# Moving the key transposes, the value order, the key weighting and the last gates of an mLSTM layer between slots

## The chip, the cores and the metric

The kernel runs on one core of a Trainium2 chip. The metric is the device time of one execution in microseconds (us). The engines are TensorE (PE for its matmuls, PEld for its weight loads), VectorE (DVE), ScalarE (ACT), GpSimd (POOL) and SyncE (SP, which issues the transfers). Each engine works through a queue of its own in order.

## The reference

The program is two layers of a diffusion backbone over 512 latent and 256 context tokens of width 1024. The first layer is attention, the second a bidirectional chunkwise mLSTM; a convolutional feed-forward block follows each. The change lies in the mLSTM alone:

```
qk, v, o, g = split(h @ w_in)
q, k = split(silu(dwconv(qk)))                 # 8 heads of 64; k is scaled by 64 ** -0.5
# per head and direction, chunk by chunk, with gates i, f and running maximum m:
s   = (q @ k.T) * exp(logw - m)
num = w_inter * (C @ q) + s @ v                # v has 128 columns a head
den = w_inter * (n @ q) + sum(s)
h   = num / max(|den|, exp(-m))
C   = decay * C + sum(w * v * k)               # the state; n likewise
# the context gives only the first state
out = (rmsnorm(h_forward + h_backward) * sigmoid(o)) @ w_out
```

## The kernel before

Every fp32 product is split into a high and a low part, so that each matrix product is three matmuls (high by high, and the two mixed ones). `split` makes the parts: ScalarE writes the high one, VectorE the low one.

The mLSTM (`odd`) first computes the gate projections and their scans, the projections of head pair 0 and the output gates of heads 0 and 1. Then a loop over 43 slots `k` interleaves the stages of eight heads. Here a token tile is 128 tokens; tiles 0 to 3 are latent, 4 and 5 are context.

- `m_intra(h)`, slot 4h: decay matmuls into a double bank ("exps"), eight exponentials on ScalarE, the score matmuls into bank T ("psT"), their product on VectorE, and the split into `Dh` and `Dl` (`Dl` on GpSimd).
- `m_state(h)`, slot 4h+2: GpSimd weights the transposed keys of the head (`kw`, from `kt`), they are split into `kh` and `kl`, 18 matmuls make the sums of the six token tiles (first the two context tiles, then 0, 1, 2, 3), two ScalarE copies and six VectorE steps make the states, and they are split into `Sh` and `Sl`.
- `m_inter(h, q)`, slot 4h+4+q: eight matmuls for token tile q, drained by two VectorE operations.
- `m_norm`, `m_scale`, `m_out`: slots 4h+7, 4h+8 and 4h+10; VectorE work, then four transposes into bank T and the product with the gate.

Between these the list `fill` places the projections of the next pairs hp = 1, 2, 3 (`proj`): `qk(0)`, the queries, at slot 8hp-5; `qk(1)`, the keys, at 8hp-3; and the values two token tiles at a time, `v(0)`, `v(2)`, `v(4)`, at 8hp-1, 8hp and 8hp+1. `qk(1)` ends with six transposes of the convolved and activated keys (`cy`) and their copy `kt`. The gates of heads 2 to 7 (`gate(h)`: 24 matmuls into bank U, then a tanh) are at slots 10, 12, 18, 20, 26 and 28. From slot 31 on the first output projection (`out_first`) fills in.

The written order gives the priorities. The framework that builds the queues may place an instruction ahead of earlier written ones that are not ready, and adds all waits; on the chip each queue then runs in its fixed order.

Buffers that matter: two double banks of tag "S" are shared by the decay products, the state, the inter results and the key transposes. The projections alternate between banks U and R. `kt`, `kw`, `kh`, `kl`, `Dh`, `Dl`, `Sh` have one buffer each. The values of two pairs fit at a time.

Of the kernel before, what the change touches and what calls it, by code (L numbers as in the profile page):

```python
# [9 lines left out]
F32 = mybir.dt.float32  # L10
# [10 lines left out]
NL, NX, T = 512, 256, 768  # L21
# [11 lines left out]
class Kernel:  # L33
# [838 lines left out]
    def odd(self, hh, hl, OT, RP, HP, xs):  # L872
        nc, i = self.nc, self.i
# [4 lines left out]
        oh = RP.tile([128, 16], F32R, tag="onehot", name="onehot")  # L878
# [14 lines left out]
        MX = RP.tile([128, NL], F32R, tag="MX", name="MX")  # L893
        Y, WI, EM = [RP.tile([128, NT, 2, 8], F32, tag=t, name=t) for t in ("Y", "WI", "EM")]
        SW = RP.tile([128, 6, 2, 8], F32, tag="SW", name="SW")
        DEC = RP.tile([128, 16, 3], F32, tag="DEC", name="DEC")

        QP = self.QP = self.tc.alloc_tile_pool(name="qk1", bufs=1, reuse_waits="tile")
# [13 lines left out]
        def proj(hp, pd):  # L912
            def qk(w01):
                ch, segs = ((hp, [(0, NL)]), (4 + hp, [(0, NL), (NL, NX)]))[w01]
                w = self.weights(i["w_mqk"][ch], KD, 128)
                yq = QP.tile([128, T], F32, tag="cy", name="cy", bufs=1)
                tiles = [QP.tile([128, NL], F32R, tag=f"{'qk'[w01]}{j}", name="qk", bufs=2 - w01) for j in range(2)]
                if w01:
                    pd["kl"] = self.kl
                pd["qk"[w01]] = tiles  # L920
                for t0, m in segs:
                    ps = self.B(pd["tags"])
                    self.fm([(ps[:, 0:m], t0, m)], w, H, KD)
                    y = yq[:, t0:t0 + m]
                    self.conv(y, [ps[:, 0:m]], [cw[:, j, ch:ch + 1] for j in range(3)], cbs[:, ch:ch + 1], [(0, m)])

                    th = QP.tile([128, NL], F32, tag="tmp", name="th", bufs=1)[:, 0:m]
                    nc.scalar.activation(th, y, AF.Tanh, scale=0.5)
                    nc.vector.scalar_tensor_tensor(y, th, 1.0, y, op0=ADD, op1=MUL)
                    for j, (a, b) in enumerate(((slice(0, 64), slice(64, 128)), (slice(64, 128), slice(0, 64)))):  # L930
                        if t0:
                            break
                        t = tiles[j][:, t0:t0 + m]
                        if w01 == 0:
                            nc.scalar.mul(t[a], y[a], 0.5)
                            nc.vector.scalar_tensor_tensor(t[b], y[a], 0.5, f32(t[a]), op0=MUL, op1=SUB)
                        else:
                            nc.scalar.mul(t[a], y[a], 0.0625)
                            nc.gpsimd.tensor_scalar(t[b], y[a], 0.0625, 1.0, op0=MUL, op1=MUL)
                            nc.vector.scalar_tensor_tensor(self.kl[j][a, t0:t0 + m], y[a], 0.0625, f32(t[a]), op0=MUL, op1=SUB)  # L940
                if w01:

                    ps = self.A("kt")
                    for t in range(6):
                        nc.tensor.transpose(ps[:, t * 128:(t + 1) * 128], yq[:, t * 128:(t + 1) * 128], self.ident)
                    pd["kt"] = QP.tile([128, 6, 128], F32, tag="kt", name="kt", bufs=1)
                    nc.scalar.mul(pd["kt"].rearrange("p t c -> p (t c)"), ps[:, 0:T], 0.0625)

            def v(t):
                if t == 0:  # L950
                    pd["wv"] = self.weights(i["w_mv"][hp], KD, 256)

                    pd["v"] = [[QP.tile([128, 6, 130], F32R, tag=f"V{x}", name="V", bufs=4) for x in "hl"] for _ in range(2)]
                    for v2 in pd["v"]:
                        for x, val in zip(v2, (1.0, 0.0)):
                            nc.gpsimd.memset(f32(x[:, :, 128:130]), val)
                ps = self.B(pd["tags"])
                for e in range(2):
                    self.tm(ps[:, 256 * e:256 * e + 256], pd["wv"], H, KD, t + e)
                ps = ps.rearrange("p (t j c) -> p t j c", t=2, j=2)  # L960
                for j, (vh, vl) in enumerate(pd["v"]):
                    self.split(vh[:, t:t + 2, 0:128], vl[:, t:t + 2, 0:128], ps[:, :, j])

            return [lambda: qk(0), lambda: qk(1)] + [lambda t=t: v(t) for t in (0, 2, 4)]

        heads = [{} for _ in range(8)]

        def gate(h, tags="U"):
            ps = self.B(tags)
            self.fm([(ps, 0, NL)], self.weights(i["w_mo"][h], KD, 128), H, KD)  # L970
            t = heads[h]["gate"] = QP.tile([128, NL], F32, tag="gt", name="gt", bufs=3)
            nc.scalar.activation(t, ps, AF.Tanh, scale=0.5)

        with self.tc.tile_pool(name="gates", bufs=1, reuse_waits="tile") as GP:
# [9 lines left out]
            w = self.weights(i["w_mg"], KD, 128)  # L984
            ps = self.A("gates")
# [6 lines left out]
            pds = [dict(tags="UR" if hp else "TURO") for hp in range(4)]  # L992
# [31 lines left out]
            c = GP.tile([64, 6], F32, name="c")  # L1024
# [56 lines left out]
        fill = [[] for _ in range(43)]  # L1081
        for hp in range(1, 4):
            f = proj(hp, pds[hp])
            for c, w in ((-5, f[0:1]), (-3, f[1:2]), (-1, f[2:3]), (0, f[3:4]), (1, f[4:5])):
                fill[8 * hp + c] += w
        for h in range(2, 8):
            fill[4 * h + 2 - (h % 2) * 2].append(lambda h=h: gate(h))

        og = RP.tile([128, KD], F32, tag="og", name="og")
        nc.sync.dma_start(og, i["ml_og"])  # L1090
# [36 lines left out]

        dirs = [heads, pds, oh, MX, Y, WI, EM, SW, DEC]
        for k in range(43):
            for st, at in ((self.m_intra, 0), (self.m_state, 2)):  # L1130
                if k >= at and (k - at) % 4 == 0 and (k - at) // 4 < 8:
                    st((k - at) // 4, MP, *dirs)
            for f in fill[k]:
                f()
            q = k - 4
            if 0 <= q < 32:
                self.m_inter(q // 4, q % 4, MP, *dirs)
                if q % 4 == 3:
                    self.m_norm(q // 4, MP, *dirs)
            if q >= 4 and (q - 4) % 4 == 0 and (q - 4) // 4 < 8:  # L1140
                self.m_scale((q - 4) // 4, MP, *dirs)
            if q >= 6 and (q - 6) % 4 == 0 and (q - 6) // 4 < 8:
                self.m_out((q - 6) // 4, OT, *dirs)
# [30 lines left out]
            nc.gpsimd.tensor_tensor(wl[:, dr], w[:, dr], f32(wh[:, dr]), op=SUB)  # L1174
        heads[h]["w"] = (wh, wl)

    def m_state(self, h, pool, heads, pds, oh, MX, Y, WI, EM, SW, DEC):

        nc = self.nc
        pd, j = pds[h // 2], h % 2  # L1180
        a = slice(64 * j, 64 * j + 64)
        kw = pool.tile([128, 6, 2, 64], F32, tag="kw", name="kw", bufs=1)
        nc.gpsimd.tensor_tensor(kw, pd["kt"][:, :, a].unsqueeze(2).to_broadcast([128, 6, 2, 64]),
                                SW[:, :, :, h:h + 1].to_broadcast([128, 6, 2, 64]), op=MUL)
        kh, kl = [pool.tile([128, 6, 2, 64], F32R, tag=f"kw{x}", name="kw" + x, bufs=1) for x in "hl"]
        self.split(kh, kl, kw)
        vh, vl = pd["v"][j]
        ps = self.A("state")
        C = []
        for z, blocks in enumerate(((4, 5), (0,), (1,), (2,), (3,))):  # L1190
            c0 = z * 130 if z < 3 else 512 + (z - 3) * 130
            C.append(ps[:, c0:c0 + 130])
            m = 0
            for t in blocks:
                for x, y in ((kh, vh), (kl, vh), (kh, vl)):
                    nc.tensor.matmul(C[z], x[:, t].rearrange("p d c -> p (d c)"), y[:, t],  # L1196
                                     start=m == 0, stop=m == 3 * len(blocks) - 1)
                    m += 1
        S = pool.tile([64, 4, 2, 130], F32, tag="S", name="S", bufs=1)
        nc.scalar.copy(S[:, 0, 0], C[0][0:64])  # L1200
        nc.scalar.copy(S[:, 3, 1], C[0][64:128])
        for z in range(3):
            nc.vector.scalar_tensor_tensor(S[:, z + 1, 0], S[:, z, 0], DEC[0:64, h, z:z + 1], C[1 + z][0:64],
                                           op0=MUL, op1=ADD)
            nc.vector.scalar_tensor_tensor(S[:, 2 - z, 1], S[:, 3 - z, 1], DEC[0:64, 8 + h, z:z + 1], C[4 - z][64:128],
                                           op0=MUL, op1=ADD)
        Sh, Sl = pool.tile([128, 4, 2, 130], F32R, tag="Sh", name="Sh", bufs=1), self.Sl[j]
        nc.scalar.copy(Sh[0:64], S)
        nc.scalar.copy(Sh[64:128], S)
        nc.vector.tensor_tensor(Sl[a], S, f32(Sh[0:64]), op=SUB)  # L1210
        heads[h]["S"] = (Sh, Sl)
# [317 lines left out]
```

## Time and the profile before

| what | value |
|---|---|
| median of 3 timed runs | 1759.9 us |
| lowest, highest | 1757.61, 1760.34 us |
| profiled execution | 1755.66 us |
| its span, first to last instruction | 1753.9 us |
| mean granted TensorE clock | 0.992 |
| TensorE, VectorE, ScalarE, GpSimd busy | 96%, 71%, 42%, 16% |

The slots lie between about 1115 and 1360 us of the span. The granted clock is given as a share of TensorE's full 2.4 GHz; its lower level is 1.2 GHz.

### The profile page before, as it was taken

Reading aid. Unit: us, or ns where it says so; the run is one execution under the profiler, and the core shown is the slowest. Engines: PE = TensorE matmul, PEld = TensorE weight load, DVE = VectorE, ACT = ScalarE, POOL = GpSimd, SP = SyncE. Lnnn points to the kernel's source line nnn. Section 1 sums busy time; section 2 is a strip of 40 time slices with the busy share of each in tenths; the row PEclk is TensorE's granted clock in tenths of the full one; section 3 lists DMA queues with packets and bytes.
Section 4 is the critical chain, followed back from the end, with each engine's and each line's share of the span. In section 5 each row is a group of like instructions: output and inputs, shape, how many; then the busy total and the mean of one; then the engine's idle time right before and its main releaser. Section 6 shows DMA issues by size and latency. Waiting matters only on the chain.

```text
span 1753.9 us, 25295 instructions
## 1 busy us (share of the span) xinstructions
PE 1675.1 (96%) x9622; PEld 1436.4 (82%) x9622; DVE 1246.6 (71%) x2308; ACT 732.6 (42%) x1362; POOL 282.9 (16%) x330
## 2 busy tenths in 40 slices
PE   7998898999999999999999989999999899999998
PEld 2787787888878888888888877788787798888887
DVE  7988889987787586675858457868778854444444
ACT  4326788986242132221312135645553532232231
POOL 0352545552130000000000015112110300000000
PEclk9998999999999999999999999999999999999999
DMA  8450000005344343342424121111112132322332
GB/s 314 127 165 24 10 12 13 13 1 209 104 142 144 99 146 119 128 149 94 150 82 143 62 97 49 61 49 37 61 44 102 61 109 96 97 97 98 98 100 88
DMA packets 67169, 166.28 MB, mean 95 GB/s; under 512 B 8164, under 2 KB 30692, under 8 KB 66664
## 3 DMA queue, kind: packets, MB, share of 16 engines
q1 hardware_dynamic: 67044, 164.66, 28.6%
q8 instruction: 76, 1.25, 0.3%
q14 instruction: 45, 0.37, 0.1%
q10 hardware_dynamic: 4, 0.01, 0.0%
HBM read 160.44 MB, written 4.20 MB: 94 GB/s over the span
## 4 chain that ended last, share of the span: by engine, by line
PE 72%; DVE 13%; ACT 7%; POOL 4%; issue 3%; DMA 0%; POOLq 0%; DVEq 0%; ACTq 0%
PE psS L85 31%; PE psT L349 7%; PE psU L349 7%; PE psU L85 4%; PE psR L85 3%; PE psT L85 2%; PE psO L349 2%; PE psR L349 2%; PE S L430 2%; ACT p L438 1%; PE psO L475 1%; POOL hl L287 1%; DVE junk L138 1%; PE state L1196 1%; PE psR L95 1%
## 5 line engine op out<-in xcount | busy, mean ns | idle before, releaser
L85 PE MATMUL psS<-hl,wh 128*128 128x512 f32 (+1 forms) x992 | 347.3, 351 | 4.4 <-POOL hl L287 4.3
L85 PE MATMUL psS<-hh,wh 128*128 128x512 f32 (+1 forms) x992 | 346.3, 350 | 0.4 <-ACT hh L283 0.4
L85 PE MATMUL psS<-hh,wl 128*128 128x512 f32 (+1 forms) x992 | 346.1, 349 | 0.0
L42 ACT CAST wh<-wr 128x1024 fp32r<-128x1024 f32 (+2 forms) x187 | 193.5, 1036 | 357.4 <-PE psO L349 141.3
L43 DVE TENSOR_TENSOR wl<-wr,wh 128x1024 fp32r<-128x1024 f32 (+2 forms) x187 | 228.6, 1223 | 43.3 <-ACT wh L42 42.8
L85 PEld LDWEIGHTS psS<-hl,wh 128*128 128x128 f32 x992 | 186.4, 188 | 32.9 <-POOL hl L287 7.1
L85 PEld LDWEIGHTS psS<-hh,wh 128*128 128x128 f32 x992 | 186.5, 188 | 26.5 <-ACT hh L283 0.9
L85 PEld LDWEIGHTS psS<-hh,wl 128*128 128x128 f32 x992 | 186.5, 188 | 25.5
L297 DVE SCALAR_TENSOR_TENSOR y<-psS,fcw,y 128x511 f32<-128x511 f32 (+1 forms) x60 | 39.5, 658 | 145.5 <-ACT y L295 145.5
L138 DVE CUSTOM_DVE_ANT_0 y<-ar,cb 128x1024 f32<-128x1024 f32 x112 | 136.6, 1220 | 0.3 <-DMA ar<-in_ada 0.3
L295 ACT ACTIVATE y<-psS,fcb,fcw 128x512 f32<-128x512 f32 (+1 forms) x60 | 40.3, 705 | 207.2 <-PE psS L85 207.2
L267 POOL TENSOR_TENSOR sa<-sa,sq 128x256 f32<-128x256 f32 (+1 forms) x18 | 18.3, 1017 | 643.8 <-ACT sq L266 643.8
L384 DVE SCALAR_TENSOR_TENSOR X<-psU,mod,X 128x512 f32<-128x512 f32 (+1 forms) x69 | 48.0, 696 | 89.4 <-PE psU L349 78.9
L441 POOL TENSOR_SCALAR p<-p,rs 128x768 f32<-128x768 f32 (+1 forms) x96 | 73.9, 776 | 114.7 <-DVE rs L440 74.1
L138 DVE CUSTOM_DVE_ANT_0 junk<-ar,cb 128x1024 f32<-128x1024 f32 x64 | 82.6, 1291 | 0.4
L349 PE MATMUL psT<-ah,wh 128*128 128x512 f32 (+1 forms) x184 | 71.6, 389 | 2.2 <-DVE X L384 1.2
L349 PE MATMUL psU<-ah,wh 128*128 128x512 f32 (+1 forms) x184 | 71.4, 388 | 1.2 <-DVE X L384 1.2
L331 DVE TENSOR_TENSOR y<-y,psS 128x512 f32<-128x512 f32 (+1 forms) x60 | 34.1, 597 | 52.5 <-PE psS L85 52.4
L349 PE MATMUL psU<-ah,wl 128*128 128x512 f32 (+1 forms) x184 | 71.0, 386 | 0.0
L349 PE MATMUL psT<-ah,wl 128*128 128x512 f32 (+1 forms) x184 | 71.0, 386 | 0.0
L349 PE MATMUL psT<-al,wh 128*128 128x512 f32 (+1 forms) x184 | 70.9, 385 | 0.0
L349 PE MATMUL psU<-al,wh 128*128 128x512 f32 (+1 forms) x184 | 70.7, 384 | 0.0
(661 smaller groups left out, 4317.6 us busy)
## 6 DMA issues: line engine op xcount, KB each, us to landing
ar<-in_ada SPq DMA_DIRECT2D x88, 512.0 KB, 3.5
wr<-in_wup SPq DMA_DIRECT2D x88, 512.0 KB, 3.4
wr<-in_wdn SPq DMA_DIRECT2D x44, 512.0 KB, 3.4
pr<-in_adak SPq DMA_DIRECT2D x8, 512.0 KB, 5.3
wr<-in_w_out SPq DMA_DIRECT2D x8, 512.0 KB, 3.5
wr<-in_w_mqk SPq DMA_DIRECT2D x8, 512.0 KB, 3.4
wr<-in_w_mv SPq DMA_DIRECT2D x8, 512.0 KB, 4.2
wr<-in_w_mo SPq DMA_DIRECT2D x8, 512.0 KB, 3.4
```

The lines of the kernel that those rows point to most:

```text
L42: nc.scalar.copy(hi, src)
L43: nc.vector.tensor_tensor(lo, src, f32(hi), op=SUB)
L85: nc.tensor.matmul(ps, a, b[:, k, x0:x0 + n], start=i == 0, stop=i == 3 * nk - 1)
L138: nc.vector.tensor_tensor_reduce(out, raw, self.cb[:, c], 1.0, 0.0, MUL, ADD, self.mraw[l][:, n, c:c + 1])
L267: (nc.vector if k % 2 else nc.gpsimd).tensor_tensor(sa[k % 2], sa[k % 2], sq, op=ADD)
L295: nc.scalar.activation(y[:, t0:t0 + n], p, AF.Identity, bias=b, scale=w[1])
L297: nc.vector.scalar_tensor_tensor(y[:, t0 + 1:t0 + n], p[:, 0:n - 1], w[0], y[:, t0 + 1:t0 + n], op0=MUL, op1=ADD)
L331: nc.vector.tensor_tensor(y[:, t0:t0 + n], y[:, t0:t0 + n], p, op=MUL)
L349: nc.tensor.matmul(ps[:, 0:n], x[:, off:off + 128], y[:, t0:t0 + n], start=m == 0, stop=m == 3 * nf - 1)
L384: self.nc.vector.scalar_tensor_tensor(X[:, o, t0:t0 + n], ps[:, 0:n], self.mod[l][:, g0 + o, c:c + 1], X[:, o, t0:t0 + n], op0=MUL, op1=ADD)
L430: nc.tensor.matmul(s[:, c0:c0 + n], q[:, q0:q0 + 128], k[:, k0 + c0:k0 + c0 + n], start=m == 0, stop=m == len(passes) - 1)
L441: nc.gpsimd.tensor_scalar(p[:, 0:nk], p[:, 0:nk], r, 1.0, op0=MUL, op1=MUL)
```

## The change

Four moves, all inside the slots; no computation is added or left out.

1. The key transposes and their copy leave `qk(1)` and become a step `kt` of their own, at slot 8hp-1, two slots later, after the first values. For pair 0 they come after all its values.
2. The values are made in the order tiles 4 and 5, 0 and 1, 2 and 3.
3. The weighting and splitting of a head's keys leaves `m_state` (slot 4h+2) for a step `m_kw` at slot 4h+1.
4. Gates 6 and 7 go from slots 26 and 28 to 28 and 30; those of heads 2 to 5 stay.

```diff
                 if w01:
-                    ps = self.A("kt")
-                    for t in range(6):
-                        nc.tensor.transpose(ps[:, t * 128:(t + 1) * 128], yq[:, t * 128:(t + 1) * 128], self.ident)
-                    pd["kt"] = QP.tile([128, 6, 128], F32, tag="kt", name="kt", bufs=1)
-                    nc.scalar.mul(pd["kt"].rearrange("p t c -> p (t c)"), ps[:, 0:T], 0.0625)
+                    pd["yk"] = yq
+
+            def kt():
+                ps = self.A("kt")
+                for t in range(6):
+                    nc.tensor.transpose(ps[:, t * 128:(t + 1) * 128], pd["yk"][:, t * 128:(t + 1) * 128], self.ident)
+                pd["kt"] = QP.tile([128, 6, 128], F32, tag="kt", name="kt", bufs=1)
+                nc.scalar.mul(pd["kt"].rearrange("p t c -> p (t c)"), ps[:, 0:T], 0.0625)
 
             def v(t):
-                if t == 0:
+                if t == 4:
                     pd["wv"] = self.weights(i["w_mv"][hp], KD, 256)
...
-            return [lambda: qk(0), lambda: qk(1)] + [lambda t=t: v(t) for t in (0, 2, 4)]
+            return [lambda: qk(0), lambda: qk(1)] + [lambda t=t: v(t) for t in (4, 0, 2)] + [kt]
...
-            for c, w in ((-5, f[0:1]), (-3, f[1:2]), (-1, f[2:3]), (0, f[3:4]), (1, f[4:5])):
+            for c, w in ((-5, f[0:1]), (-3, f[1:2]), (-1, f[2:3]), (-1, f[5:6]), (0, f[3:4]), (1, f[4:5])):
                 fill[8 * hp + c] += w
-        for h in range(2, 8):
-            fill[4 * h + 2 - (h % 2) * 2].append(lambda h=h: gate(h))
+        for h, k in zip(range(2, 8), (10, 12, 18, 20, 28, 30)):
+            fill[k].append(lambda h=h: gate(h))
...
-            for st, at in ((self.m_intra, 0), (self.m_state, 2)):
+            for st, at in ((self.m_intra, 0), (self.m_kw, 1), (self.m_state, 2)):
...
-    def m_state(self, h, pool, heads, pds, oh, MX, Y, WI, EM, SW, DEC):
+    def m_kw(self, h, pool, heads, pds, oh, MX, Y, WI, EM, SW, DEC):
...
         self.split(kh, kl, kw)
-        vh, vl = pd["v"][j]
+        heads[h]["kw"] = (kh, kl)
+
+    def m_state(self, h, pool, heads, pds, oh, MX, Y, WI, EM, SW, DEC):
+        nc = self.nc
+        pd, j = pds[h // 2], h % 2
+        a = slice(64 * j, 64 * j + 64)
+        (kh, kl), (vh, vl) = heads[h]["kw"], pd["v"][j]
```

## Rows read from the trace of the kernel before

**Rows 1.** The page: busy us, share of the span and instructions of each engine.

```profile
PE 1675.1 (96%) x9622; PEld 1436.4 (82%) x9622; DVE 1246.6 (71%) x2308; ACT 732.6 (42%) x1362; POOL 282.9 (16%) x330
```

**Rows 2.** Stretches of the slots: length, busy of PE, PEld, DVE, ACT, POOL; clock; DMA.

```profile
1120.00:1300.00 180.00, 169.91 (x1162) 152.40 (x1161) 138.73 (x281) 93.71 (x208) 33.26 (x33) 1.00 0.15 48
1300.00:1319.00 19.00, 15.34 (x92) 12.67 (x90) 13.92 (x34) 12.64 (x29) 2.51 (x2) 1.00 0.31 110
1319.00:1326.00 7.00, 7.00 (x32) 6.61 (x32) 6.13 (x14) 1.03 (x3) 0.00 (x0) 0.52 0.34 117
```

**Rows 3.** TensorE's waits from 1120 to 1335: us in total, times, longest us.

```profile
PE kt L945 <- DVE cy L929: 3.8, 5, 1.1
PE state L1196 <- DVE V L43: 2.0, 3, 0.7
...
PE psT L1169 <- DVE OT L1269: 1.2, 1, 1.2
```

**Rows 4.** Timeline of TensorE, pair 2: start, us, instruction, [idle before <- releaser].

```profile
1202.50 0.36 PE L95 MATMUL psR<-wh,hh 128*128 128x256 f32 x1 [0.82 <-DVE cy L298]
...
1203.86 0.66 PE L945 MATMUL kt<-ident,cy 128*128 128x128 f32 x4 [0.54 <-DVE cy L929]
...
1207.33 0.44 PE L945 MATMUL kt<-ident,cy 128*128 128x128 f32 x2 [0.97 <-DVE cy L929]
```

**Rows 5.** Timeline of VectorE, the same stretch.

```profile
1203.11 0.69 DVE L929 SCALAR_TENSOR_TENSOR cy<-th,cy 128x512 f32<-128x512 f32 x1 [0.76 <-ACT th L928]
...
1206.85 0.43 DVE L929 SCALAR_TENSOR_TENSOR cy<-th,cy 128x256 f32<-128x256 f32 x1
...
1208.66 0.42 DVE L1233 TENSOR_TENSOR num<-num 128x260 f32<-128x260 f32 x1
```

**Rows 6.** TensorE's waits from 1090 to 1120, pair 0 and the gate arithmetic.

```profile
PE kt L945 <- DVE cy L929: 1.1, 2, 0.7
PE psR L1074 <- ACT Y L1076: 1.1, 1, 1.1
```

**Rows 7.** Timeline of TensorE around the state of head 4.

```profile
1229.70 0.22 PE L1227 MATMUL num<-V,Dh 128*128 128x130 f32 x1
...
1230.60 0.22 PE L1196 MATMUL state<-V,kwh 128*128 128x130 f32 x1
...
1231.60 0.44 PE L1196 MATMUL state<-V,kwh 128*128 128x130 f32 x2 [0.67 <-DVE V L43]
```

**Rows 8.** Timeline of VectorE: a low key split, and the value split of Rows 7.

```profile
1214.13 0.95 DVE L43 TENSOR_TENSOR kwl<-kw,kwh 128x768 fp32r<-128x768 f32 x1
...
1231.13 0.42 DVE L43 TENSOR_TENSOR V<-psR,V 128x256 fp32r<-128x256 f32 x1
```

**Rows 9.** The chain that ended last, around state 6: start us, us, what.

```profile
1294.49 2.00 PE state L1196 x16
1296.50 5.67 PE psU L85 x24
```

**Rows 10.** Timeline of GpSimd, pair 2.

```profile
1208.77 1.50 POOL L1183 TENSOR_TENSOR kw<-kt,SW 128x768 f32<-128x768 f32 x1 [3.21 <-ACT kt L947]
1215.16 1.50 POOL L1183 TENSOR_TENSOR kw<-kt,SW 128x768 f32<-128x768 f32 x1 [4.89 <-DVE kwl L43]
...
1216.88 2.55 POOL L1174 TENSOR_TENSOR Dl<-D,Dh 128x512 fp32r<-128x512 f32 x2
```

**Rows 11.** Timeline of ScalarE: the key copies of pair 2, and gate 6.

```profile
1207.81 0.81 ACT L947 ACTIVATE kt<-kt 128x768 f32<-128x768 f32 x1 [1.71 <-PE kt L945]
...
1302.19 0.60 ACT L972 ACTIVATE gt<-psU 128x512 f32<-128x512 f32 x1 [4.38 <-PE psU L85]
```

**Rows 12.** Timeline of TensorE after gate 7.

```profile
1316.31 0.52 PE L1268 MATMUL psT<-ident,hn 128*128 128x128 f32 x3 [0.98 <-DVE hn L1262]
1318.30 0.30 PE L1196 MATMUL state<-V,kwh 128*128 128x130 f32 x1 [1.48 <-DVE num L1233]
```

**Rows 13.** Timeline of TensorE: the first inter step of head 3.

```profile
1223.19 0.22 PE L1227 MATMUL num<-V,Dh 128*128 128x130 f32 x1
```

## Prediction

> **What bounds the kernel now.** I read the page first: TensorE is busy 1675.1 us (96% of the span) and VectorE 71% [rows 1]. TensorE sets the end, so an edit that changes no matmul can only give back time in which TensorE stands still or runs slowly. The table by stretches then shows where that is in the mLSTM slots: 169.91 of 180 us busy from 1120 to 1300, 15.34 of 19 from 1300 to 1319, and from 1319 to 1326 a granted clock of 0.52, nearly all of it at the lower level (1.2 GHz) [rows 2]. The list of TensorE's waits says what each hole waited for: from 1120 to 1335 there are 3.8 us before the key transposes (five waits), 2.0 before the state matmuls on the value split (three), and one of 1.2 before a score matmul on a transpose bank [rows 3]; the timeline adds waits of 0.82 before the values, 0.98 and 1.48, each shown below. These holes and the slow stretch are all that can be gained.
>
> **The time that the sum starts from.** The profiled execution took 1755.66 us around a span of 1753.9. The three timed runs have a median of 1759.9, 4.2 us higher. I work out differences from the profiled execution and take them off the median. About 0.2%, 3.5 us, is what a measurement of this kernel can tell from no change.
>
> **Key transposes two slots later.** The same six transposes, one ScalarE copy per pair and the same weighting on GpSimd are made, four of the transposes in 0.66 us [rows 4]; nothing is added or removed. In the pair at 1200 us, four transposes start at 1203.86 after a wait of 0.54 and two at 1207.33 after 0.97 [rows 4]. They wait for the second silu product on VectorE, at 1203.11 (latent) and 1206.85 (context) [rows 5]. Matmuls queue in order, so values already hoisted before them, and the state behind them, wait too. Two slots later these products are over: about 3.8 us over pairs 1 to 3 is given back. Pair 0 has the same wait, 1.1 us [rows 6], but I count nothing for it: the gate arithmetic then holds TensorE again on its own, 1.1 us for Y alone [rows 6], and that VectorE chain is not shortened. If it had slack, 1.1 us would be added.
>
> What is late next is a bank. The values write bank R, which the convolution (cy, L298) frees; the 0.82 us wait at 1202.50 [rows 4], which stands in pairs 2 and 3, has nothing to do with the keys, and the new first value piece uses the same bank. But without the transposes the program now offers the inter step (0.9 us, from 1229.70 to 1230.60 in [rows 7]) and the next state (2.0 us of matmuls [rows 9], its keys weighted long before) ahead of it, so I take half of the 1.6 us, 0.8; bounds 0 and 1.6. The Trainium skill ("Perfetto Trace Analysis", Optimization Strategy) says that the same gap repeating on the engine that should be saturated can mean that no buffer is free for the next tile. By that rule the holes would be a matter of banks, and this item and the one before it would give 0 and not 4.6 us; the rows name VectorE's product for the larger part and a bank for the smaller, so they bear it out only there.
>
> New waits: the transposes now stand between the inter steps, the state and the decay products of slots 15 and 16, all of which share two double banks. The inter result made between the two groups of transposes is drained by two VectorE steps of 0.42 us, the second of which ran as late as 1208.66 [rows 5]. One late drain per pair costs TensorE 0.8 us where no value matmuls are at hand, 0 where they are; I charge 0.8 for each of three pairs, 2.5 us; bounds 0 and, where both drains in a pair come late, 5.
>
> **Context values first.** Each state begins with the two context tiles, which now come last out of the projection. TensorE started two matmuls and then waited 0.67 us for the split [rows 7], made on VectorE at 1231.13 [rows 8] behind a weight split. After the change the last split made belongs to tiles 2 and 3, whose matmuls are the last six of eighteen: the twelve before them take about 1.3 us (two thirds of the 2.00 us of sixteen [rows 9]), over twice the wait. So 0.65 us for each of three pairs goes: 2.0 us. Nothing else waits for the early tiles, since the inter steps of the pair begin two slots later. Lower bound 0, if the weight splits move behind it again.
>
> **Weighted keys one slot ahead.** In the rows, GpSimd's weighting already runs right after the copy (1208.77 after a copy of 0.81 from 1207.81 [rows 10, 11]) and long before the state of that head at 1230.6. Written order was not what held it, so I count 0. In exchange the keys now come later: copy 0.81 [rows 11], weighting 1.50 and two splits of at most 0.95 each [rows 8] are 4.2 us, and between the new transposes and the state lie two value pieces, each with the columns of a gate (48 of 256 against 24 of 512), 5.67 us [rows 9]. They fit; the cover is 11.3 us, and if it were gone the 4.2 us would stand ahead of each even head's state.
>
> **Last gates later.** Gate 6 moves from slot 26 to 28 and gate 7 from 28 to 30; each is 24 matmuls, 5.67 us, one tanh and one weight piece, loaded and split in the same order as before among the other pieces. Today gate 6 runs at 1296.5, and after gate 7 nothing is left to cover: TensorE waits 0.98 us for the normalized head 5, then 1.48 for an inter bank [rows 12], after 1.2 for the transpose bank [rows 3]. That is 3.65 us. ScalarE also stands idle 4.38 us behind gate 6's tanh [rows 11], with head 6's state copies queued behind it. With the gate gone from slot 26, both inter steps of head 5 follow its state directly, its normalization starts earlier, and gate 7 lies where the last two waits are. In place of the hole at the end there is one at slot 26: after a state the two S copies and six VectorE steps hold the bank. The gate can be pulled ahead there, as value matmuls are today in front of the transposes [rows 4]. I take 2.5 of the 3.65; bounds 0 and 3.65. The new position has its own price: gate 7's bank U is next wanted by the first output piece, which may wait for the tanh of 0.60: 0.8 us with the hand-over.
>
> The clock follows from this. A mean of 0.52 from 1319 to 1326 [rows 2] is 6.7 of 7 us at the lower level, right after the waits of 0.98 and 1.48 [rows 12]. Half of the 6.7 us, 3.4, is lost there. If the gate fills those waits I expect the clock to stay up: 3.4 us; bounds 0 and 3.4. The Trainium skill ("TensorE: Matmul & The Clock Gate", What's actually happening) says that the slow clock is the default state and that activity releases it. By it a hole that merely moves to slot 26 would bring its own slow stretch, and this item would be 0 and not 3.4; the granted clock of 0.52 right after the holes [rows 2] agrees with the rule, but no row shows slot 26 without its gate.
>
> **The sum.** 3.8 + 0.8 + 2.0 + 2.5 + 3.4 = 12.5 us gained, 2.5 + 0.8 = 3.3 charged: 9.2 us. 1755.66 becomes 1746.5 by the profile, and the median 1759.9 becomes **1750.7**. With all gains at their upper bounds and no charge: 3.8 + 1.1 + 1.6 + 2.0 + 3.65 + 3.4 = 15.6, or 1744.3.
>
> **Rivals.** *The waits change place.* VectorE is busy 138.73 of 180 us in these slots [rows 2] and its work is the same; if the holes come back as waits for banks, and the hole of the tail moves to slot 26 with its slow stretch, then what is left is the value split, 2.0, and a quarter of the transposes, 1.0: 3.0 us, 1756.9. For it: the bank waits in the list; against it: VectorE has over 40 us of free time in that stretch. *Nothing moves.* The framework already places instructions other than in written order (the value matmuls ahead of the transposes, the early weighting), so that it may arrive at much the same queues: 1759.9. Against it: the transposes do stand before a product that they wait for. *GpSimd's queue, slower.* The second head's weighting stands on GpSimd ahead of the low part Dl and waits for the low key split; today it waited 4.89 us, ran at 1215.16, and Dl followed at 1216.88 for 2.55 [rows 10]. Inter 3,0 wants Dl at 1223.19 [rows 13], 3.8 us later. With keys made some 3.7 us later (about 1211.5 against 1207.81: the values may start at 1202.5 [rows 4], a value piece, two inter steps and the transposes add 5.7 + 0.9 + 0.9 + 0.7 to 1210.7, and the banks take some) that margin is used up; it decides once the split that ran at 1214.13 [rows 8] comes after 1217.9. If it falls behind the head normalization, about 5 us beyond that, each of three pairs waits 5 us: 15 less 9.2 gained, 1765.7. Against it: the weighting need not stay ahead of Dl on the queue.
>
> **How the numbers follow.** Forecast 0.50, between 6 and 14 us gained (1746 to 1754). Waits that change place 0.28, between 1 and 5.5 us gained, a little over half of it beyond 3.5. Nothing moves 0.10. GpSimd's queue 0.10. The remaining 0.02 I give to the faster side beyond these. Faster by over 0.2%: 0.50 + 0.17 + 0.02 = 0.69; within: 0.11 + 0.10 = 0.21; slower 0.10. The range reaches from just below the upper bound of all gains, 1743.5, to just past no change, 1760.5; outside lie mainly GpSimd's case and a little of the run-to-run spread.
>
> **What would show it.** Right: no wait of the transposes on the silu product in pairs 1 to 3; no wait of the state on a value split; gate 7 between state 7 and the last inter steps of head 6; no fall of the granted clock after head 5's transposes. Wrong: new waits of the inter, decay or transposes on VectorE drains of over 1 us each; a slow stretch after slot 26; Dl ending after inter 3,0 could have begun; or the six transposes still meeting their product because the framework pulls them forward.

## The result, and the profile after

The change makes the kernel slower: a median of 1768.8 us (five runs, 1766.84 to 1774.14) against 1758.9 us (1757.61 to 1760.34) of the kernel before in the same rounds, a ratio of 1.0062 with a 95% interval of 1.0048 to 1.0076. Forecast were 1750.7 us and a range up to 1760.5; the time lies outside it, on the slower side, to which the prediction gave a chance of 0.10. The profiled execution took 1768.76 us, with a span of 1767.0 and a mean granted clock of 0.984 (before 1753.9 and 0.992). Below, "before" is some 1758 us: each session of experiments timed it again (1758.5, 1758.2, 1758.1, 1758.1), and each experiment has five rounds against it; the medians are of 5 to 12 runs.

The page of the kernel after; it answers to [rows 1]:

```profile
PE 1684.8 (95%) x9622; PEld 1445.2 (82%) x9622; DVE 1250.0 (71%) x2308; ACT 731.4 (41%) x1362; POOL 282.5 (16%) x330
```

TensorE runs the same 9622 instructions and is busy 9.7 us longer; the span is 13.1 us longer. So about 3.4 us are more standing still, and the rest is slower running. The stretches of [rows 2], after (length, busy of PE, PEld, DVE, ACT, POOL, clock, DMA), then shorter ones behind three holes:

```profile
1120.00:1300.00 180.00, 168.25 (x1136) 152.85 (x1136) 137.41 (x269) 90.65 (x202) 32.03 (x33) 0.96 0.13 42
1300.00:1319.00 19.00, 14.00 (x84) 11.33 (x83) 17.09 (x42) 9.79 (x26) 2.86 (x2) 0.97 0.15 46
1319.00:1326.00 7.00, 6.90 (x25) 6.33 (x26) 2.77 (x8) 0.53 (x2) 0.00 (x0) 0.50 0.14 51
...
1204.00:1212.00 8.00, 3.79 (x18) 3.75 (x18) 7.71 (x17) 2.98 (x7) 1.23 (x2) 0.58 0.21 62
1272.00:1280.00 8.00, 6.71 (x44) 6.74 (x45) 5.60 (x13) 0.33 (x2) 0.00 (x0) 0.79 0.17 50
1316.00:1330.00 14.00, 10.99 (x39) 9.48 (x39) 5.67 (x16) 0.53 (x2) 0.00 (x0) 0.63 0.09 29
```

Before, the clock was whole from 1120 to 1319; now it falls in the middle of the slots. TensorE's waits from 1060 to 1380, after:

```profile
PE num L1237 <- DVE num L1243: 11.2, 4, 4.2
PE psU L1121 <- DVE oh L46: 3.2, 3, 1.8
PE state L1206 <- DVE num L1243: 3.0, 1, 3.0
...
PE psT L1077 <- DVE sn L1051: 1.7, 1, 1.7
```

The waits that the change was forecast to remove are gone: no `kt` and no state on a value split. In their place stand 11.2 us of inter steps (`num`) that wait for the drain of an earlier inter step, and 3.0 us of state 7 on the same drain.

**The hole of a pair.** TensorE in pair 2:

```profile
1201.94 0.22 PE L1206 MATMUL state<-V,kwh 128*128 128x130 f32 x1
...
1203.79 0.28 PE L1206 MATMUL state<-V,kwh 128*128 128x130 f32 x1
1208.28 0.44 PE L1237 MATMUL num<-V,Dh 128*128 128x130 f32 x1 [4.21 <-DVE num L1243]
1208.52 0.41 PE L1237 MATMUL num<-V,Dl 128*128 128x130 f32 x1
```

The same hole in pair 3, and the first value matmul behind it:

```profile
1273.29 0.30 PE L1237 MATMUL num<-V,Dh 128*128 128x130 f32 x1 [3.92 <-DVE num L1243]
...
1275.68 0.56 PE L95 MATMUL psR<-wh,hh 128*128 128x256 f32 x1
```

VectorE and ScalarE in the time of pair 2's hole:

```profile
1203.64 0.69 DVE L929 SCALAR_TENSOR_TENSOR cy<-th,cy 128x512 f32<-128x512 f32 x1 [0.76 <-ACT th L928]
1204.25 0.48 DVE L297 SCALAR_TENSOR_TENSOR cy<-psU,mcw,cy 128x255 f32<-128x255 f32 x1
1204.76 0.48 DVE L298 SCALAR_TENSOR_TENSOR cy<-psU,mcw,cy 128x255 f32<-128x255 f32 x1
1205.16 0.42 DVE L1242 TENSOR_TENSOR num<-num,WI 128x260 f32<-128x260 f32 x1
1205.56 1.79 DVE L940 SCALAR_TENSOR_TENSOR kl<-cy,qk 64x512 fp32r<-64x512 f32 x2
1207.37 0.42 DVE L929 SCALAR_TENSOR_TENSOR cy<-th,cy 128x256 f32<-128x256 f32 x1
1207.72 0.42 DVE L1243 TENSOR_TENSOR num<-num 128x260 f32<-128x260 f32 x1
```

```profile
1204.89 1.28 ACT L938 ACTIVATE qk<-cy 64x512 fp32r<-64x512 f32 x2
1206.20 0.42 ACT L928 ACTIVATE th<-cy 128x256 f32<-128x256 f32 x1
1206.52 0.24 ACT L1210 COPY S<-state 64x130 f32<-64x130 f32 x1
```

TensorE makes an inter step, then the state, and wants the next inter step, which needs one of the two "S" double banks. One is held by the inter step until its second drain (L1243), the other by the state until the S copies and the VectorE steps behind them. The inter step's matmuls end about where the state starts, at 1201.94, but its first drain (L1242) runs only at 1205.16: a silu product and the convolution of the context keys (L929, L297, L298) stand ahead of it on VectorE. The second drain runs 2.1 us after the first ended, because the low part of the keys (`kl`, 1.79 us) and another silu product stand between the two. Before the change the second drain was no earlier (1208.66 [rows 5]); there TensorE had the values and the transposes to run meanwhile. Now the values, whose matmuls could have filled the time, are queued behind that inter step. The hole is 1.82 us in pair 1; in slot 26, left without its gate, it is 1.27. In pairs 2 and 3 the clock then falls: `num` on `V,Dl` takes 0.41 us at 1208.52, where it takes 0.27 at the upper level.

**The tail.** TensorE around state 7, then VectorE and ScalarE:

```profile
1315.13 0.50 PE L85 MATMUL psU<-hh,wh 128*128 128x512 f32 x1 [0.58 <-ACT gt L975]
...
1319.10 0.45 PE L1206 MATMUL state<-V,kwh 128*128 128x130 f32 x1 [3.01 <-DVE num L1243]
1319.34 0.42 PE L1206 MATMUL state<-V,kwl 128*128 128x130 f32 x1
...
1334.56 0.73 PE L1121 MATMUL psU<-oh,wh 128*128 128x512 f32 x2 [0.72 <-DVE oh L46]
```

```profile
1316.72 0.96 DVE L43 TENSOR_TENSOR wl<-wr,wh 128x768 fp32r<-128x768 f32 x1
1317.60 0.42 DVE L1242 TENSOR_TENSOR num<-num,WI 128x260 f32<-128x260 f32 x1
...
1318.54 0.42 DVE L1243 TENSOR_TENSOR num<-num 128x260 f32<-128x260 f32 x1
```

```profile
1330.46 0.60 ACT L975 ACTIVATE gt<-psU 128x512 f32<-128x512 f32 x1 [6.71 <-PE psU L85]
1330.95 3.17 ACT L45 ACTIVATE oh<-OT,og 128x512 fp32r<-128x512 f32 x5
```

Gate 7 starts after gate 6's tanh, and only three of its 24 matmuls stand ahead of state 7. State 7 waits 3.01 us for the drains of the inter steps just before it, which stand behind the head normalization and a weight split on VectorE. Then it and the other 21 matmuls of gate 7 run until 1330.26, most of that time at the lower level (the clock from 1316 to 1330 is 0.63). The splits of the finished heads (`oh`) for the output projection go into the buffers of the layer's input, which gate 7 is the last to read; they start behind its tanh, and the output projection waits for them.

At the end of state 6 the kernel is 4.5 us late (its last matmul ends at 1300.98; the chain of [rows 9] gives 1296.49), at the end of the span 13.1. The pairs and the tail both lose.

### The profile page after: what moved, and what is told of

It is laid out like the page before. It is cut to its first block, busy times and chain, and to the rows that moved or that the text cites. A ratio compares the mean times of both kernels' runs of the same rounds, so it can differ in the third digit from the quotient of the medians.

```text
span 1767.0 us, 25294 instructions
## 1 busy us (share of the span) xinstructions
PE 1684.8 (95%) x9622; PEld 1445.2 (82%) x9622; DVE 1250.0 (71%) x2308; ACT 731.4 (41%) x1362; POOL 282.5 (16%) x330
## 4 chain that ended last, share of the span: by engine, by line
PE 75%; DVE 12%; ACT 6%; POOL 4%; issue 3%; DMA 0%; POOLq 0%; DVEq 0%; ACTq 0%; SPq 0%
PE psS L85 30%; PE psT L349 7%; PE psU L349 7%; PE psU L85 4%; PE psR L85 3%; PE psT L85 2%; PE psR L95 2%; PE psO L349 2%; PE psR L349 2%; PE S L430 2%; PE psO L475 1%; PE psU L95 1%; POOL hl L287 1%; PE psR L1121 1%; DVE junk L138 1%
## 5 line engine op out<-in xcount | busy, mean ns | idle before, releaser
L297 DVE SCALAR_TENSOR_TENSOR y<-psS,fcw,y 128x511 f32<-128x511 f32 (+1 forms) x60 | 39.5, 658 | 145.4 <-ACT y L295 145.4
```

Source lines behind the costliest of these rows:

```text
L297: nc.vector.scalar_tensor_tensor(y[:, t0 + 1:t0 + n], p[:, 0:n - 1], w[0], y[:, t0 + 1:t0 + n], op0=MUL, op1=ADD)
```

## The experiments

### One part alone

**Keys alone** (the values' order, gates and weighting put back):

```
-            return [qk(0), qk(1)] + [v(t) for t in (4, 0, 2)] + [kt]
+            return [qk(0), qk(1)] + [v(t) for t in (0, 2, 4)] + [kt]
-        for h, k in zip(range(2, 8), (10, 12, 18, 20, 28, 30)): fill[k]...
+        for h in range(2, 8): fill[4 * h + 2 - (h % 2) * 2]...
-            ... (self.m_intra, 0), (self.m_kw, 1), (self.m_state, 2)
+            ... (self.m_intra, 0), (self.m_kw, 2), (self.m_state, 2)
```

> Key transposes two slots later, nothing else changed. Theory of the banks: without the transposes no value matmuls are pulled in between the inter steps of slots 13 and 14, so that the second inter step waits for a bank that VectorE drains late; three waits of 2 to 4 us in pairs 1 to 3, two of them with a slow clock after them: 4 to 9 us slower than before. Rival, the loss is all in the tail (gates): the transposes' 3.8 us are given back, 2 to 4 us faster.

1772.8 us, ratio 1.0076 (1.0064 to 1.0089): the transposes' new place by itself is enough to lose 14.3 us, more than the whole change does and more than the 4 to 9 us that were expected.

**Values alone** (context values first; all else put back):

```
-            return [qk(0), qk(1)] + [v(t) for t in (0, 2, 4)]
+            return [qk(0), qk(1)] + [v(t) for t in (4, 0, 2)]
```

> Value order 4, 0, 2 alone. As predicted: the state no longer waits for a value split, three waits of 0.65 us go, about 2 us faster, and no new wait of TensorE. Rival, the split's place is taken by another wait: within 1 us of before.

1755.6 us, ratio 0.9978 (0.9968 to 0.9988), 3.0 us gained. This part does what was forecast, and a little more.

**Gates alone** (gates 6 and 7 later; all else put back):

```
-        for h in range(2, 8): fill[4 * h + 2 - (h % 2) * 2]...
+        for h, k in zip(range(2, 8), (10, 12, 18, 20, 28, 30)): fill[k]...
```

> Gates 6 and 7 two slots later, nothing else changed. As predicted: the tail's waits of 3.65 us and its slow stretch go, 3 to 5 us faster. Theory from the trace after: the splits of the head outputs stand on ScalarE behind the tanh of gate 7, the output pieces wait for them, state 7 waits about 3 us for a bank, the slow stretch stays or grows: 4 to 8 us slower than before.

1764.1 us, ratio 1.0028 (1.0015 to 1.0041). The loss of 5.6 us is what the second theory expected. The waits of the tail are those of the whole change, 3.0 before state 7 and 3.2 for `oh`; whether the waits for `oh` make the loss is tested below.

**Keys and values** (the change with its gates put back):

```
-        for h, k in zip(range(2, 8), (10, 12, 18, 20, 28, 30)): fill[k]...
+        for h in range(2, 8): fill[4 * h + 2 - (h % 2) * 2]...
```

> The change with gates 6 and 7 left where they were before. Theory of the banks: the keys' loss less 2 us for the value split, 2 to 7 us slower than before and 4 to 8 us faster than the whole change. Rival, the loss is all in the tail: 4 to 6 us faster than before.

1763.5 us, ratio 1.0033 (1.0023 to 1.0044). Its waits of inter steps on the drain, from 1060 to 1380:

```profile
PE num L1237 <- DVE num L1243: 10.0, 3, 4.2
```

The two halves lose 5.0 and 5.6 us, the whole some 10: they add up and are taken apart below. The keys and the values do not add up: with the keys moved, the values' order is worth 9.3 us (1772.8 against 1763.5) and not 3.0. In "keys alone" the state still waits 2.9 us for value splits, and in "keys and values" not at all; what makes up the rest was not tested. The weighting has no run of its own: put back alone, or moved alone, it leaves the instructions of all five queues in the same order.

### The hole of the pairs

Three changes to "keys and values". **Busy in the hole:** fourteen 128x512 matmuls into bank O, which nobody reads, in slots 14 and 22.

```
+            if k in (14, 22): self.warm(14)     # matmul(psO, identb, tri[0]), 14 times
```

> Keys and values as changed, gates as before; 14 matmuls that nothing reads are added into an idle bank after the states of slots 14 and 22, where TensorE waits 4.2 and 3.9 us for the drain. They take about 3.2 us, so that they fit the hole and keep TensorE busy in it. Theory of the clock (most of the loss is the slow stretch after the hole): the slow stretches near 1207 and 1272 go, 4 to 7 us faster than the same kernel without them. Rival, the hole itself is the loss because VectorE sets the pace: within 1.5 us of the kernel without them.

**Values a slot earlier:**

```
-            for c, w in (..., (-1, f[2:3]), (-1, f[5:6]), ...):
+            for c, w in (..., (-2, f[2:3]), (-1, f[5:6]), ...):
```

> Keys and values as changed, gates as before, but the first value piece one slot earlier, ahead of the second inter step. Theory of the banks: TensorE has 5.7 us of value matmuls while VectorE drains the first inter step, so the waits of 10 us in pairs 1 to 3 fall to 2 or less and no slow stretch follows; 6 to 10 us faster than with the piece in its slot, 1 to 5 us faster than before. Rival, VectorE is too far behind in any order: the wait moves to the next inter step, within 3 us of the kernel with the piece in its slot.

**Drains first:** the two drains of each inter step get a higher priority in the framework's ordering.

```
+        with self.tc.high_priority(offset=600):
             nc.vector.tensor_tensor(num[:, q], both(o), WI..., op=MUL)
             nc.vector.tensor_tensor(num[:, q], num[:, q], both(ps[:, 0:260]), op=ADD)
```

> Keys and values as changed, gates as before, but both VectorE drains of an inter step get priority over the projection's work on VectorE. The second drain then stands one key step earlier on the queue, about 1.3 us. Theory of the banks: the 4.2 us waits fall by 1 to 2 us each, with less slow clock; 2 to 5 us faster than the same kernel with the drains in written order. Rival, the clock alone counts and the holes stay long enough: within 1.5 us.

| kernel | median us | ratio to before (95%) | waits of inter steps on the drain |
|---|---|---|---|
| keys and values | 1763.5 | 1.0033 (1.0023 to 1.0044) | 10.0 |
| busy in the hole | 1759.1 | 1.0006 (0.9997 to 1.0014) | 3.9 |
| values a slot earlier | 1754.2 | 0.9976 (0.9968 to 0.9985) | 0.9 |
| drains first | 1760.0 | 1.0010 (1.0001 to 1.0018) | 5.8 |

Against "keys and values" these are gains of 4.4, 9.3 and 3.5 us, each within what its theory expected.

With the values a slot earlier, TensorE goes from the state straight into 48 value matmuls and from these into the inter step:

```profile
1204.87 0.28 PE L1206 MATMUL state<-V,kwh 128*128 128x130 f32 x1
1204.98 0.33 PE L95 MATMUL psR<-wh,hh 128*128 128x256 f32 x1
...
1210.53 0.27 PE L95 MATMUL psR<-wh,hl 128*128 128x256 f32 x1
1210.64 0.22 PE L1237 MATMUL num<-V,Dh 128*128 128x130 f32 x1
```

VectorE does nothing sooner in this run: the second drain (L1243) starts at 1208.77, with `kl` and the silu product ahead of it as in the change. TensorE has other work until then.

The busy matmuls leave a wait of 1.20 us, and the clock stays up behind it (0.27 us for the same `V,Dl` matmul):

```profile
1207.03 3.20 PE L1228 MATMUL warm<-tri,identb 128*128 128x512 bf16 x14
1211.42 0.30 PE L1244 MATMUL num<-V,Dh 128*128 128x130 f32 x1 [1.20 <-DVE num L1250]
1211.56 0.27 PE L1244 MATMUL num<-V,Dl 128*128 128x130 f32 x1
```

The stretch from 1190 to 1300 in "keys and values" and with the busy matmuls (columns as above):

```profile
1190.00:1300.00 110.00, 101.73 (x692) 93.67 (x691) 85.59 (x176) 53.63 (x129) 17.76 (x19) 0.94 0.14 43
1190.00:1300.00 110.00, 107.83 (x745) 95.64 (x743) 89.61 (x181) 56.79 (x133) 19.85 (x20) 1.00 0.14 43
```

The clock is 0.94 in the first and 1.00 with the busy matmuls, which compute nothing that is used and give back 4.4 us. So the lower clock is a cost of its own. The cause of the hole is the order: real work in the same place takes away wait and fall, 9.3 us, and turns the loss into a gain. Earlier drains shorten the waits and give back 3.5.

### The gates

From the kernel before, **gate 7 alone** (slot 30, gate 6 at 26) and **gate 6 alone** (slot 28, beside gate 7):

```
+        for h, k in zip(range(2, 8), (10, 12, 18, 20, 26, 30)): fill[k]...   # gate 7 alone
+        for h, k in zip(range(2, 8), (10, 12, 18, 20, 28, 28)): fill[k]...   # gate 6 alone
```

> The kernel before with gate 7 alone moved, from slot 28 to 30; gate 6 stays at 26. Theory of the buffer: the split head outputs are written into the buffer of the layer's input, which gate 7 reads last, so that they can't start before it has run; the output pieces then wait about 3 us for them, and state 7's hole stays empty: 3 to 6 us slower than before, all of the loss of moving both gates. Rival, the loss comes from the empty slot 26: within 1.5 us of before.

> The kernel before with gate 6 alone moved from slot 26 to slot 28; gate 7 stays in slot 28, so both are offered there. Moving both gates cost 5.6 us (about 1764), moving gate 7 alone nothing (1758.5). Theory 'empty slot 26': the loss comes from slot 26, which has nothing left to put between the state and the second inter step: wait of that inter step on the bank's second drain over 1 us, a slow stretch after it, and 3 to 6 us slower than before (1761.5 to 1764.5). Rival 'it takes both': the loss needs gate 7's later place too (few matmuls ahead of state 7, and the output head splits behind its tanh), so this one alone stays within 1.5 us of before.

1758.5 us, 1.0000 (0.9991 to 1.0009), and 1758.2 us, 1.0003 (0.9994 to 1.0011). The first expectation was wrong, and of the second the rival was right: neither gate 7's later place with its waits for `oh` (3.2 us in "gate 7 alone" as well) nor an empty slot 26 loses by itself. State 7 in "gate 7 alone", in "gate 6 alone", and in "gates alone":

```profile
1315.36 0.30 PE L1207 MATMUL state<-V,kwh 128*128 128x130 f32 x1 [0.82 <-DVE num L1244]
```

```profile
1320.24 0.30 PE L1207 MATMUL state<-V,kwh 128*128 128x130 f32 x1 [0.91 <-DVE num L1244]
```

```profile
1316.66 0.45 PE L1207 MATMUL state<-V,kwh 128*128 128x130 f32 x1 [3.00 <-DVE num L1244]
1316.90 0.42 PE L1207 MATMUL state<-V,kwl 128*128 128x130 f32 x1
```

One gate left in its place, or both in one slot, leaves state 7 a short wait; only the two moves together leave it one of 3.0 us with the fall behind it. From 1310 to 1340 the clock is 0.94, 0.94 and 0.82; it was 0.89 in the kernel before. Two more runs put that to the test: fourteen unread matmuls in slot 30 ahead of state 7 of "gates alone", and the whole change with gate 7 back at slot 28.

```
+            if k == 30: self.warm(14)                                          # the first
-        for h, k in zip(range(2, 8), (10, 12, 18, 20, 28, 30)): fill[k]...   # the second
+        for h, k in zip(range(2, 8), (10, 12, 18, 20, 28, 28)): fill[k]...
```

> Both gates later alone (1764.1 us), with fourteen 128x512 matmuls that nobody reads, in the idle bank O, in slot 30 ahead of state 7, where TensorE stands still for 3.0 us and the clock then lies at the lower level for 10.2 us. Theory 'clock in the tail': the slow stretch is the larger part of what the two gates together lose; with TensorE busy in the hole it goes and the time is 3.5 to 5.1 us less, 1759 to 1760.5. Rival 'waits': the waits for the output heads' split (3.2 us) and the 3.0 us themselves are the loss, and the time stays within 1.5 us of 1764.

> The whole change with gate 7 put back into slot 28, beside gate 6. Theory 'two gates together': the gates' loss comes from gate 7's matmuls being queued behind state 7, which is then reached with the banks not drained; with gate 7 ahead of it, as in the kernel with gate 6 moved alone (no loss), the time is that of keys and values alone, 1762 to 1765. Rival 'empty slot 26': with the keys and values moved as well, slot 26's bank wait of 1.3 us and what follows it stay, and at most 1.5 us of the 5 come back: 1767 or more.

The busy tail gives 1760.9 us (1.0012, 1.0003 to 1.0021): 3.3 us of the 5.6 come back, a little less than expected. Gate 7 put back gives 1763.7 us (1.0034, 1.0023 to 1.0044): all that the gates cost in the whole change, 5 us, with state 7's wait at 0.91, as the theory "two gates together" had it.

### How much is clock, how much is waiting

**The whole change with fourteen unread matmuls** in slots 14, 22 and 30:

```
+            if k in (14, 22, 30): self.warm(14)
```

> The whole change (1768.8 us) with fourteen such matmuls in slots 14, 22 and 30, that is in the holes of pairs 2 and 3 and ahead of state 7. No wait of the change is taken away. Theory 'clock': nearly the whole loss is the lower clock after these holes; the gains in the two places add up (4.4 for the pairs, measured on the version without the later gates, and 3.5 to 5 in the tail) and the time is 1759 to 1761, level with the kernel before. Rival 'waits': at most the 4.4 us of the pairs come back, 1764 or more.

1766.5 us (1.0043, 1.0028 to 1.0059): 2.3 us came back. That is the rival's range (1764 or more) and not the theory's 1759 to 1761. But the run is no clean test of the two. Its fourteen matmuls stand ahead of the slot's state, while those of "busy in the hole" stand behind it, right ahead of the wait. And here the clock falls behind what is left of the wait:

```profile
1202.57 3.19 PE L1228 MATMUL warm<-tri,identb 128*128 128x512 bf16 x14
...
1208.92 0.30 PE L1244 MATMUL num<-V,Dh 128*128 128x130 f32 x1 [1.20 <-DVE num L1250]
1209.06 0.37 PE L1244 MATMUL num<-V,Dl 128*128 128x130 f32 x1
1209.23 0.63 PE L1244 MATMUL num<-V,Dh 128*128 128x130 f32 x2
```

The remedy held little of the clock (a mean of 0.9850 against 0.9832 in the change), so the run says little on what the clock costs. The spread of the runs says more. In the 21 runs of the kernel before in that session the span is 1753.1 to 1754.4 us at a granted clock of 0.991 and 1759.6 at 0.985; the fit is 1.0 us per 0.001 (0.7 to 0.75 in three other sets of 18 to 35 runs). By 0.7 to 1.0 us and the mean clocks of the runs, I estimate the clock's part:

| from, to | mean clocks | clock's part, us | measured, us |
|---|---|---|---|
| before, the change | 0.9885, 0.9832 | 3.7 to 5.3 | +9.8 |
| before, keys and values | 0.9885, 0.9810 | 5.3 to 7.5 | +5.0 |
| before, gates alone | 0.9885, 0.9873 | 0.8 to 1.2 | +5.6 |
| keys and values, busy | 0.9810, 0.9859 | 3.4 to 4.9 | -4.4 |
| keys and values, values earlier | 0.9810, 0.9865 | 3.9 to 5.5 | -9.3 |
| gates, busy tail | 0.9873, 0.9897 | 1.7 to 2.4 | -3.3 |

By this estimate the clock's part is all of what the keys and values lose. Their profiled execution points the same way:

```profile
PE 1684.0 (96%) x9622; PEld 1446.9 (82%) x9622; DVE 1250.0 (71%) x2308; ACT 731.9 (42%) x1362; POOL 282.1 (16%) x330
```

Of its span of 1761.4 us TensorE stands still for 77.4, before for 78.8 (1753.9 less 1675.1): the same matmuls run 8.9 us longer, and the waits in sum have not grown. For the gates alone the two readings differ. The estimate gives the clock 0.8 to 1.2 of 5.6 us, while in the profiled execution, the slowest of seven, the matmuls run 9.3 us longer and TensorE stands still only 1.4 us longer; how much of the gates' loss is clock stays open.

The estimate is coarse, and no run holds the clock still. "Gate 7 put back" takes 1763.7 us at a mean clock of 0.9849 and "keys and values" 1763.5 at 0.9810; by the same rate they should lie 2.7 to 3.9 us apart. One difference lies at the gate arithmetic, where both wait 1.71 us near 1112: from 1090 to 1130 the clock is 0.96 in the one and 0.87 in the other, so that slow time there may cost less than the rate says.

### Pair 0, the tail before, and a better version

**Pair 0's transposes put back** into its projection, in "values a slot earlier"; **ten unread matmuls ahead of state 7 in the kernel before**; and both together:

```
-            for f in p0[0:2] + p0[5:6] + p0[2:5]:     # becomes, in the first and the third:
+            p0 = proj(0, pds[0])
+            for f in p0[0:2] + p0[5:6] + p0[2:5]:     # kt right after qk(1)
+            if k == 30: self.warm(10)                 # in the second and the third
```

> The version with the values a slot earlier (1754.2 us), with pair 0's transposes put back into its projection. Theory: in that version, as in the change, pair 0's transposes come right ahead of the gate arithmetic, so the wait for the normalized gate rows (0.77 us before, 1.71 with the change) grows and the clock falls near 1112 us; put back, that stretch goes and the time is 1 to 3 us less, 1751 to 1753. Rival: the gate arithmetic holds TensorE by itself, the 1.1 us wait at the transposes comes back, and the time is within 1 us of that version.

> The kernel before with ten 128x512 matmuls that nobody reads, in the idle bank O, in slot 30 ahead of state 7, where TensorE waits 0.98 and 1.48 us and the clock then lies at the lower level for nearly 7 us. Theory: the lower level after these waits costs half of its 6.8 us; if TensorE is kept busy there it is saved, less what the ten matmuls (about 0.22 us each at the upper level) need beyond the waits: 1.5 to 3.4 us faster than before. Rival: the matmuls only put the waits off, or the fall stays: within 1 us of before, or slower by up to 2.2.

> The version of the previous entry but one (values a slot earlier, pair 0's transposes back) with the ten unread matmuls of the previous entry. If the two gains stand in different places they add up: 1749 to 1752, 6 to 9 us faster than before. Rival: the tail of this version no longer has the holes of before (its heads reach it otherwise), and the ten matmuls cost their own time: 1753 to 1756.

The first gives 1753.5 us (0.9974, 0.9965 to 0.9982), 0.7 less than without it, which its interval does not tell from nothing, as its rival had it. The second gives 1757.4 us (0.9998, 0.9989 to 1.0006): no gain, as the rival had it. The two waits before state 7 became ten matmuls of 2.33 us and a wait of 0.80, and the fall came later, by half its length. The third gives 1751.4 us (0.9968, 0.9956 to 0.9980), the fastest here and in the range expected if the gains add up; but its interval overlaps the first one's, so what the ten matmuls add there is not shown. They are dead work; "values a slot earlier" with pair 0 put back gains 4.6 us without any.

## Why the prediction was wrong, by its steps

Both halves of the forecast failed, by about as much. The items of the keys and values come to 4.1 us gained in the prediction, and 5.0 were lost; those of the gates and the clock come to 5.1 gained, and 5.6 were lost.

**Key transposes, +3.8: the waits went, the time did not.** No transpose waits for the silu product in pairs 1 to 3. But the waiting transposes had made the framework pull the values ahead of them, so TensorE had work while VectorE was busy ([rows 4]: values from 1202.50, transposes at 1203.86). With the transposes gone, the values fell behind the next inter step.

**Bank R, +0.8: at its upper bound as a wait.** The waits on the convolution (1.6 us, two, in "values alone") are gone after the change; what they are worth in time was not measured.

**New waits, -2.5: the first step that failed.** It named the mechanism, "one late drain per pair costs TensorE 0.8 us where no value matmuls are at hand", and mis-sized it: 1.82, 4.21 and 3.92 us, 10.0 in the three pairs against 2.5, twice the upper bound of 5. The price came from two drains of 0.42 us; what stands ahead of them and between them on VectorE (a silu product and a convolution ahead; `kl`, 1.79 us, and a silu product between) was not counted. The lower clock behind the new holes was put at nothing. The place was wrong too: the hole is behind the state ahead of the transposes (slots 13 and 14), not in slots 15 and 16.

**Context values first, +2.0: right.** The waits are gone, and the part by itself gives 3.0.

**Weighted keys a slot ahead, 0: right.** The queues are the same with and without it.

**Last gates, +2.5 and -0.8: the second step that failed, wrong in sign.** The step expected gate 7 "where the last two waits are"; only three of its matmuls came ahead of state 7, and two waits of 0.98 and 1.48 us [rows 12] became one of 3.0. The 0.8 was for a wait of the first output piece on bank U; the waits came from the input buffers that gate 7 keeps (3.2 us), and with the same waits "gate 7 alone" is no slower than before.

**The clock, +3.4: wrong in sign.** It was lost, 3.7 to 5.3 us by the estimate above. Its condition, that the gate fills the waits, did not hold, and its lower bound of 0 was no bound: the step looked at the one fall of before [rows 2] and not at new ones behind new holes. The Trainium skill ("TensorE: Matmul & The Clock Gate", What's actually happening) says that the slow clock is the default and activity releases it, and the prediction drew from it that a hole that moves brings its slow stretch along. The trace agrees: 0.58 from 1204 to 1212 and 0.79 from 1272 to 1280, behind holes of 4.21 and 3.92 us. It did not follow every hole: behind the waits of 1.82 us in pair 1 and 1.27 in slot 26 `num` on `V,Dl` takes 0.28 and 0.27 us, the upper level.

**Pair 0, 0: about right.** The wait of 1.1 us at its transposes [rows 6] went; the one for the normalized gate rows (`sn`) grew from 0.77 to 1.71 us. Putting the transposes back changes the time by 0.7 us.

**The rivals.** "The waits change place" had the mechanism, bank waits and a slow stretch that moves, but let a gain of 3.0 us stand: it let holes come back at the size of those removed, and the waits on drains in the pairs came to 10.0 us against 3.8 [rows 3]. Its argument against, VectorE's 40 us of free time, says nothing on when VectorE is free. The rule of the Trainium skill beside the first item ("Perfetto Trace Analysis", Optimization Strategy), that a repeating gap on the engine that should be busy can mean that no buffer is free, spoke for this rival and would have made the gain of the transposes and the bank 0; the trace agrees with it after the change, with a gap in each of three pairs in which an inter step waits for its bank. The bank is late because of VectorE's queue and TensorE's order, and in "values a slot earlier" another order alone takes these gaps down to 0.9 us. "GpSimd's queue" named the slower side for a reason that did not come: no inter step waits for `Dl` in the list of waits.

## What to carry to other kernels

An instruction that waits in an ordered queue may be what makes the framework put other work ahead of it: before moving it away, ask what TensorE will run in its old place, and which bank the next step in the queue needs. Price a late drain by all that stands ahead of it on its engine in that stretch, not by its own length; and count each new hole of some microseconds with the clock behind it. Two moves that cost nothing each can lose together when each had left the other's work as cover.

## What the runs showed of the hardware

The clock does not answer to a hole of one length in one way. In slot 26 the same work stands ahead of the wait in the whole change and in the whole change with the unread matmuls of slots 14, 22 and 30. Behind a wait of 1.27 us the clock stayed up in the first; behind one of 1.26 us it fell in the second:

```profile
1302.38 0.27 PE L1237 MATMUL num<-V,Dl 128*128 128x130 f32 x1
```

```profile
1301.44 0.42 PE L1244 MATMUL num<-V,Dl 128*128 128x130 f32 x1
```

Two executions of one and the same kernel differ by up to 0.008 in their mean granted clock and by 7.6 us in span ("gate 7 alone"; the kernel before by 0.006 and 6.8 us), which is more than most single edits here were worth; a difference of that size needs many runs.
